# Low parts of the second layer's query and gate weights by ScalarE and an adding transfer, and the rotary swap by ScalarE

## The chip, the cores and the metric

The kernel runs on one core of a Trainium2 chip. A core has a matrix engine (TensorE, PE in the profile, with its weight loads as PEld), a vector engine (VectorE, DVE), an activation engine (ScalarE, ACT), a general engine (GpSimd, POOL), a queue engine that starts transfers (SyncE, SP) and 16 DMA engines. Each engine works through its own instructions in order; semaphores tie them together. Tiles lie in SBUF (128 partitions), matmul results in PSUM, inputs and outputs in HBM.

The metric is the time of one execution in microseconds (us), the median of several runs. A profiled execution gives the trace; its span runs from the first to the last instruction.

## The reference

Two layers work on x, 1024 tokens of 1024 features, each ending in a weighted residual and a layer norm. The first is gated linear attention with four heads. The second projects one shared set of keys and values and then, for eight query heads and three groups, runs attention over a dilated window:

```
for u in 0..7:                       # query heads, 128 wide
    for g, (window, d) in ((128,1), (512,4), (2048,16)):
        q = rope(x @ wB[u, g])       # 1024 tokens x 128
        k, v = K[u // 4, g], V[u // 4, g]
        o[g], lse[g] = attention of token t over t, t-d, t-2d, ..., t-window
    o = sum over g of o[g], weighted by softmax(lse over g)
    og[u] = o * silu(x @ wB[u, 3])
out = layer_norm(alpha * x + concat(og) @ wOB)
```

where rope(q) = q * cos + swap(q) * sin, and swap exchanges the two halves of the 128 features, with a minus sign on one of them. Everything is fp32.

## The kernel before

**Numbers in two parts.** A projection is made of fp32r matmuls, a format with fewer bits that TensorE multiplies faster (512 columns in 227 ns, where 128 of plain fp32 take 112 ns). A number is split into a high part, its rounding to fp32r, and a low part, what is left; a product is high*high + high*low + low*high. `mm3` (line 642) issues these three matmuls, `proj_cols` (649) eight times three for one half (512 tokens) of a projection, `project` (655) both halves for one piece of weights and hands each finished PSUM bank to an evacuation function.

**Weights.** A piece is 128 by 1024 numbers, 512 KB. `load_w` (625) starts its transfer on SP into `wf` (two buffers), ACT copies it to the high part `wh` (three buffers), and DVE or GpSimd subtracts `wf - wh` into the low part `wl` (three buffers). There are 100 pieces of this full size, 32 of them from wB (queries and gates of the eight heads).

**The second layer** (`layer_b`). First values and keys are projected; then for each head `q_proj` (three pieces, rotated by `rope`), `g_proj` (one piece, silu through a tanh), `scores` and `attend`. `rope` (1194) makes acc * cos on DVE, two products of 64 partitions each on DVE for the swapped halves with sin, and one add on DVE or GpSimd that writes the result in the group's order (`to_group`): group 0 in token order, group 1 as four interleaved sequences of 256, group 2 as sixteen of 64. In `scores` (1327) a block of 128 queries is the stationary operand and the keys are the moving one; group 1 has per head four products 128 wide and four 256 wide. These score products are plain fp32. The exponentials run on ACT; the merge weights of the groups (`cw`) go through small DMAs; `attend` (1415) scales P, transposes it (into `ms`), masks it into `PT` (DVE, and in part GpSimd), and multiplies by V into `po`.

**What sets the order.** The program is recorded first and then put in order by a planner of its own (`Sched`, lines 141 to 454), which also chooses the engine where the code leaves a choice: `S.vp` is DVE or GpSimd, `S.va` DVE or ACT, `S.vap` any of the three. It places operation after operation by a modelled start time and a priority, with costs from `cost` (543 to 595); loads of weights are recorded with a priority that places them early. So a change to costs or to a choice moves instructions on every engine. All of them are issued from one line, 452 (453 after the change), so the profile's groups are told apart by tiles, not lines.

Of the kernel before, what the change touches and what calls it, by code (L numbers as in the profile page):

```python
# [12 lines left out]
AF = mybir.ActivationFunctionType  # L13
# [21 lines left out]
WEIGHTS, EVAC, WARM = 3000, 1000, 4  # L35
AHEAD = 0.35
RUNS, GATHER = 0.3, 1.0


class Buf:  # L40
# [100 lines left out]
class Sched:  # L141
# [20 lines left out]
    def record(self, engs, meth, args, kw):  # L162
        a = list(args)
        outs = [v for k, v in kw.items() if k in ("out", "accum_out")]
        ins = [v for k, v in kw.items() if k not in ("out", "accum_out")]
        if "out" not in kw:
            outs.append(a[0])
            ins = a[1:] + ins
        else:
            ins += a  # L170
        outs = [v for v in outs if isinstance(v, View)]
        ins = [v for v in ins if isinstance(v, View)]
        if meth == "copy_predicated":
            ins += outs
        n = max([int(_np.prod(v.shape[1:])) for v in outs + ins if not (meth == "matmul" and v is not outs[0])] or [0])
        func = None
        if meth in ("copy", "affine", "scale"):
            func = "Copy"
        elif meth == "activation":
            func = str(a[2]).split(".")[-1]  # L180
        costs = [cost(e, meth, n, outs, ins, args, kw) + self.extra for e in engs]
        g = self.group_op
        if g is None:
            o = Op()
            o.engs, o.calls, o.reads, o.writes, o.cost = engs, [], [], [], [0.0] * len(engs)
# [12 lines left out]
        o.reads += ins  # L198
        o.writes += outs
        o.cost = [x + y for x, y in zip(o.cost, costs)]  # L200
# [53 lines left out]
    def order(self):  # L254
# [62 lines left out]
        while n_done < len(ops):  # L317
# [40 lines left out]
                    c += 1.3 if cur_set else 0.0  # L358
                    cur_set = new
            o.t0, o.eng = st, e  # L360
            if e == "SP":
                dma_free = max(dma_free, st) + c
                o.t1 = dma_free + 1.7
                free[e] = st + 0.37
            else:
                o.t1 = st + c
                free[e] = o.t1
                if o.port[o.engs.index(e)]:
                    port = o.t1
# [162 lines left out]
def shares_port(e, meth, outs, ins):  # L532

    n = sum(v.buf.pool.space is None for v in ins if int(_np.prod(v.shape[1:])) > 1)
    if e == "POOL":
        return n > 0
# [6 lines left out]
def cost(e, meth, n, outs, ins, args, kw):  # L543

    if e == "PE":
# [9 lines left out]
            return 0.12  # L555
        m = args[1].shape[1]
        return {32: 0.02, 64: 0.05}.get(m, 0.43)
    if e == "SP":
# [39 lines left out]
def trunk(tc, xT, wP, wA, wA12, wAv3, w2, wO, wK, wV0, wV12, wB, wOB, par_d,  # L598
# [23 lines left out]
        return slice(half * 512, half * 512 + 512)  # L622


    def load_w(src):
        with S.later(-WEIGHTS):
            return load_w_now(src)

    def load_w_now(src):
# [6 lines left out]
        split_hi(hi, wf)  # L636
        lo = wts.tile([128, 1024], FR, name="wl", bufs=3)
        lo = lo[:, :k * c].rearrange("p (k c) -> p k c", k=k)
        split_lo(lo, wf, hi)
        return hi, lo  # L640

    def mm3(acc, wh, wl, xh, xl, kt):
# [9 lines left out]
            xh, xl = xs[kt]  # L652
            mm3(acc, hi[:, kt, :], lo[:, kt, :], xh[:, r], xl[:, r], kt)

    def project(piece, xs, evac, halves=(0, 1)):
        w = load_w(piece)
# [519 lines left out]
    def layer_b(xs, early):  # L1176
# [14 lines left out]
        sinT = page(p0, F32, "sinT")  # L1191
        S.sync.dma_start(sinT, sin_d)

        def rope(pg, g, half, acc):
            r = hs(half)
            t1 = small("t1", "t1", 2)
            S.vector.tensor_mul(t1, acc, cosT[:, r])
            t2 = small("t2", "t2", 2)
            S.vector.tensor_mul(t2[0:64, :], acc[64:128, :], sinT[64:128, r])
            S.vector.tensor_mul(t2[64:128, :], acc[0:64, :], sinT[0:64, r])  # L1200
            S.vp.tensor_add(to_group(pg, g, half), tok_view(t1, g), tok_view(t2, g))

        K = [[page(p0, F32, f"K{c}{g}") for g in range(3)] for c in range(2)]
        V = [[None] * 3 for _ in range(2)]
# [98 lines left out]
        def q_proj(u):  # L1303
            Q = [page(p0, F32, "Q") for _ in range(3)]
            U[u]["Q"] = Q
            for g in range(3):
                project(wB[u, g], xs, lambda half, acc: rope(Q[g], g, half, acc))


        def g_proj(u):  # L1310
# [7 lines left out]
            project(wB[u, 3], xs, evac)  # L1318


        def pieces(P, g, j0):
# [4 lines left out]

        def scores(u):
            Q, Kc = U[u]["Q"], K[u // 4]
            P = {}
            sts = hp.tile([128, 2, 24], F32, name="sts", bufs=2)  # L1330
            for g in (2, 1, 0):
                step = 8 if g == 2 else 2
                for j0 in range(0, 8, step):
# [11 lines left out]
                    for j in range(j0, j0 + step):  # L1345
# [4 lines left out]
                        P[g, j] = p, o  # L1350
                        px = p[:, o:o + nk]
                        if g < 2:
                            S.tensor.matmul(sc[:, o:o + nk], Q[g][:, qc:qc + 128], Kc[g][:, kc:kc + nk],
                                             start=True, stop=True)
                        mk = rmask if g == 2 else bmask[:, 256 - nk:]

# [244 lines left out]
def _arrays(inputs):  # L1601
# [10 lines left out]
    r = np.arange  # L1612
# [36 lines left out]
    a["sin"] = c(np.concatenate([sn, -sn]))  # L1649
# [36 lines left out]
```

## Time and profile before

| | |
|---|---|
| runs | 1154.63, 1153.87, 1154.25 us; median 1154.25 |
| profiled execution | span 1152.7 us; the median lies 1.55 us above it |
| granted TensorE clock | 0.998 of full speed |
| transfers | 107.13 MB on the hardware queue, 29.6% of 16 DMA engines |
| a transfer of GpSimd's queue | none |

The profile lists busy times by engine, the share of each engine in 40 slices, the chain of work that ended last, and groups of equal instructions. In a group `wl<-wf,wh 128x1024` reads: result, operands, shape; `x39` is the count, then total busy time, mean ns of one, and the idle time before them with what ended it. The timeline has start, duration, engine, line, instruction, with the idle time before it and its releaser in brackets. A matmul's duration is longer than the distance to the next one, since they are pipelined; the distance counts.

### The profile page before, as it was taken

The page shows a single profiled execution, that of the slowest core. Times are in us where ns is not written, and L with a number is a line of the kernel's source. Part 1 is how long each engine was busy: PE and PEld are TensorE (multiplying, and loading weights), DVE is VectorE, ACT ScalarE, POOL GpSimd, SP SyncE. Part 2 cuts the span into 40 slices and gives each one's busy share as a digit, 9 for nine tenths or more (in the row PEclk, how much of TensorE's full clock was granted, in tenths as well). Part 3 has the DMA queues.
Part 4 walks back from the last instruction along what each step waited for, and adds up shares of the span by engine and source line. Part 5 has one row for each costly group of instructions (what it writes and reads, how often), then busy time and mean ns, then how long its engine had stood idle before and what let it go on. Part 6 is the DMA issues. An engine that isn't in the chain of part 4 may idle for free.

```text
span 1152.7 us, 19731 instructions
## 1 busy us (share of the span) xinstructions
PE 1142.8 (99%) x7780; PEld 975.2 (85%) x7780; DVE 820.3 (71%) x1634; ACT 449.1 (39%) x929; POOL 188.0 (16%) x139
## 2 busy tenths in 40 slices
PE   9999999999999999999999999999999999999997
PEld 9888888889988888888988888888888888888876
DVE  6286862786966699764366868686777878767678
ACT  5355431646463335311214242424222443444342
POOL 1000100112011120211020303030211312212200
PEclk9999999999999999999999999999999999999999
DMA  7211222111144365443611111121141111134544
GB/s 256 71 38 38 74 79 87 38 61 51 57 171 140 137 214 158 166 143 103 208 47 34 51 38 57 38 50 45 38 165 39 38 21 38 39 96 126 193 136 182
DMA packets 93372, 108.39 MB, mean 94 GB/s; under 512 B 43648, under 2 KB 61952, under 8 KB 93280
## 3 DMA queue, kind: packets, MB, share of 16 engines
q1 hardware_dynamic: 93280, 107.13, 29.6%
q8 instruction: 61, 1.00, 0.4%
q14 instruction: 31, 0.25, 0.1%
HBM read 85.94 MB, written 21.17 MB: 93 GB/s over the span
## 4 chain that ended last, share of the span: by engine, by line
PE 93%; DVE 4%; DMA 2%; ACT 1%; issue 1%; POOL 0%; DVEq 0%; ACTq 0%
PE acc L452 63%; PE po L452 9%; PE lv L452 8%; PE vac L452 7%; PE ms L452 4%; PE pro L452 2%; DMA wf<-in_wOB 2%; DVE rt L452 1%; DVE wl L452 1%; DVE x1l L452 0%; ACT wh L452 0%; DVE P L452 0%; DVE lnA L452 0%; ACT woh L452 0%; DVE wol L452 0%
## 5 line engine op out<-in xcount | busy, mean ns | idle before, releaser
L452 PE MATMUL acc<-x1h,wh 128*128 128x512 f32 x608 | 252.3, 415 | 0.0
L452 PE MATMUL acc<-x1h,wl 128*128 128x512 f32 x608 | 237.6, 391 | 0.0
L452 PE MATMUL acc<-x1l,wh 128*128 128x512 f32 x608 | 237.1, 390 | 0.0
L452 ACT ACTIVATE wh<-wf 128x1024 fp32r<-128x1024 f32 (+2 forms) x104 | 108.1, 1040 | 281.0 <-PE acc L452 194.8
L452 POOL TENSOR_TENSOR wl<-wf,wh 128x1024 fp32r<-128x1024 f32 x39 | 93.5, 2397 | 553.1 <-ACT wh L452 414.8
L452 ACT ACTIVATE P<-P,sts 128x128 f32<-128x128 f32 (+2 forms) x192 | 81.5, 426 | 139.6 <-DVE sts L452 139.3
L452 PEld LDWEIGHTS acc<-x1h,wl 128*128 128x128 f32 x608 | 114.1, 188 | 24.5
L452 PEld LDWEIGHTS acc<-x1l,wh 128*128 128x128 f32 x608 | 114.5, 188 | 21.3
L452 PEld LDWEIGHTS acc<-x1h,wh 128*128 128x128 f32 x608 | 114.4, 188 | 21.1
L452 DVE TENSOR_TENSOR wl<-wf,wh 128x1024 fp32r<-128x1024 f32 (+2 forms) x66 | 83.4, 1265 | 58.2 <-ACT wh L452 48.0
L452 PE MATMUL acc<-xh,wh 128*128 128x512 f32 x256 | 101.8, 397 | 0.0
L452 PE MATMUL acc<-xh,wl 128*128 128x512 f32 x256 | 99.8, 390 | 0.0
L452 PE MATMUL acc<-xl,wh 128*128 128x512 f32 x256 | 99.7, 390 | 0.0
L452 DVE TENSOR_TENSOR t<-acc,cosT 128x512 f32<-128x512 f32 x60 | 41.4, 689 | 65.7 <-PE acc L452 65.7
L452 DVE TENSOR_TENSOR t<-acc,sinT 64x512 f32<-64x512 f32 x120 | 82.5, 688 | 1.6
L452 PE MATMUL lv<-K,Q 128*64 128x64 f32 (+2 forms) x512 | 70.2, 286 | 0.0
L452 DVE CUSTOM_DVE_ANT_0 P<-lv,bmask 128x256 f32<-128x256 f32 (+1 forms) x128 | 46.7, 379 | 25.1 <-PE lv L452 23.7
L452 PEld LDWEIGHTS lv<-K,Q 128*128 128x128 f32 (+1 forms) x512 | 53.8, 163 | 10.0 <-issue 1.6
L452 PE MATMUL acc<-ogh,wh 128*128 128x512 f32 x152 | 60.1, 395 | 0.0
L452 PE MATMUL acc<-ogh,wl 128*128 128x512 f32 x152 | 59.2, 389 | 0.0
L452 PE MATMUL acc<-ogl,wh 128*128 128x512 f32 x152 | 59.2, 389 | 0.0
L452 PEld LDWEIGHTS acc<-xh,wl 128*128 128x128 f32 x256 | 48.0, 188 | 10.2
(252 smaller groups left out, 2233.4 us busy)
## 6 DMA issues: line engine op xcount, KB each, us to landing
wf<-in_wB SPq DMA_DIRECT2D x32, 512.0 KB
wf<-in_wA SPq DMA_DIRECT2D x24, 512.0 KB
wf<-in_wO SPq DMA_DIRECT2D x16, 512.0 KB
wf<-in_wOB SPq DMA_DIRECT2D x16, 512.0 KB
wf<-in_wV SPq DMA_DIRECT2D x12, 512.0 KB
res<-in_xT SPq DMA_DIRECT2D x16, 256.0 KB
x1d<-rt SPq DMA_DIRECT2D x16, 256.0 KB
out<-rt SPq DMA_DIRECT2D x16, 256.0 KB
```

What stands on the lines that cost most here:

```text
L452: getattr(handle[o.eng], meth)(*[conv(a) for a in args], **{k: conv(v) for k, v in kw.items()})
```

## The change

Four things change.

1. For the 32 pieces of wB the low part is no longer a subtraction. ACT writes the negated high part into `wl` (a copy of `wf` with scale -1, rounded to the same format), and a transfer on GpSimd's queue reads the same piece from HBM a second time and adds it to `wl`.
2. In `rope`, ACT copies the two halves of the PSUM bank, swapped, to `t2`, and one product with sin of all 128 partitions follows on DVE or GpSimd. The signs in the sin array are exchanged to suit. This holds for the keys as well.
3. Group 1 of the queries is stored in token order; `scores` reads its blocks with a step of four elements (16 bytes) as the stationary operand.
4. The planner gets costs for such transfers: 1.1 us of GpSimd (`ISSUE`) and 3.0 us until landing (`QUEUED`), and treats the target of an adding transfer as an input.

```diff
-            if e == "SP":
+            if o.calls[0][0] == "dma_start":
                 dma_free = max(dma_free, st) + c
-                o.t1 = dma_free + 1.7
-                free[e] = st + 0.37
+                o.t1 = dma_free + (1.7 if e == "SP" else QUEUED)
+                free[e] = st + (0.37 if e == "SP" else ISSUE)
...
         lo = lo[:, :k * c].rearrange("p (k c) -> p k c", k=k)
-        split_lo(lo, wf, hi)
+        if added:
+            S.scalar.activation(lo, wf, AF.Copy, scale=-1.0)
+            S.gpsimd.dma_start(lo, src, accum_op=OP.add)
+        else:
+            split_lo(lo, wf, hi)
...
-        def rope(pg, g, half, acc):
+        def rope(pg, g, half, acc, walked=(0, 1, 2)):
...
-            S.vector.tensor_mul(t2[0:64, :], acc[64:128, :], sinT[64:128, r])
-            S.vector.tensor_mul(t2[64:128, :], acc[0:64, :], sinT[0:64, r])
-            S.vp.tensor_add(to_group(pg, g, half), tok_view(t1, g), tok_view(t2, g))
+            S.scalar.copy(t2[0:64, :], acc[64:128, :])
+            S.scalar.copy(t2[64:128, :], acc[0:64, :])
+            S.vp.tensor_mul(t2, t2, sinT[:, r])
+            if g in walked:
+                S.vp.tensor_add(to_group(pg, g, half), tok_view(t1, g), tok_view(t2, g))
+            else:
+                S.vp.tensor_add(pg[:, r], t1, t2)
...
-                project(wB[u, g], xs, lambda half, acc: rope(Q[g], g, half, acc))
+                project(wB[u, g], xs, lambda half, acc: rope(Q[g], g, half, acc, (0, 2)), added=True)
...
+            Q = [Q[0], Q[1].rearrange("p (i r) -> p r i", r=4), Q[2]]
...
-                            S.tensor.matmul(sc[:, o:o + nk], Q[g][:, qc:qc + 128], Kc[g][:, kc:kc + nk],
+                            qb = Q[1][:, qc // 256, qc % 256:qc % 256 + 128] if g else blk(Q[0], j)
+                            S.tensor.matmul(sc[:, o:o + nk], qb, Kc[g][:, kc:kc + nk],
```

The planner places the second layer anew. On GpSimd, from the last rows of the first layer to the first head's attention; `x1l` is the low part of that layer's result, `PT` the masked attention weights. Before:

```order
L452 TENSOR_TENSOR x1l_4390<-rt,x1h_4373 128x512
L452 TENSOR_TENSOR x1l_4445<-rt,x1h_4430 128x512
L452 TENSOR_TENSOR wl<-wf,wh 128x1024 x12
L452 TENSOR_SCALAR P<-P,cw 128x256 x3
L452 TENSOR_TENSOR wl<-wf,wh 128x1024
L452 TENSOR_TENSOR Q<-t_6224,t_6236 128x4x8x16
L452 TENSOR_TENSOR PT<-P,ident 128x128
L452 TENSOR_TENSOR PT<-P,ident 128x256 x3
```

The same place after:

```order
L453 TENSOR_TENSOR x1l_4390<-rt,x1h_4373 128x512
L453 TENSOR_TENSOR x1l_4445<-rt,x1h_4430 128x512
L453 TENSOR_TENSOR wl<-wf,wh 128x1024 x6
L453 DMA wl<-in_wB 128x1024 x9
L453 TENSOR_TENSOR PT<-P,ident 128x128 x3
L453 DMA wl<-in_wB 128x1024
L453 TENSOR_TENSOR PT<-P,ident 128x128
L453 TENSOR_TENSOR PT<-P,ident 128x256 x3
```

GpSimd keeps its masked products and a few subtractions of key and value weights; where it subtracted for queries and gates, it issues transfers, and the scaling of P and the add into Q have left it.

On ACT, in the queries of the second head while the first head's scores end; `P,sts` is an exponential with its sum, `ew` belongs to the merge weights, `t` is a half of the swap. Before:

```order
L452 ACTIVATE th<-acc 128x512
L452 ACTIVATE P,sts<-P,sts 128x256 x6
L452 ACTIVATE wh<-wf 128x1024
L452 ACTIVATE ew<-ew 128x24
L452 ACTIVATE wh<-wf 128x1024
L452 ACTIVATE P<-P,cw 128x128
```

The same place after:

```order
L453 ACTIVATE P,sts<-P,sts 128x256 x6
L453 ACTIVATE t_6022<-acc 64x512 x2
L453 ACTIVATE P,sts<-P,sts 128x256
L453 ACTIVATE wh<-wf 128x1024
L453 ACTIVATE wl<-wf 128x1024
L453 ACTIVATE t_6077<-acc 64x512 x2
L453 ACTIVATE ew<-ew 128x24
L453 ACTIVATE t_6124<-acc 64x512 x2
L453 ACTIVATE wh<-wf 128x1024
L453 ACTIVATE wl<-wf 128x1024
```

Each high part has its negation behind it, and each half projection two copies that empty its PSUM bank.

On PE, at the first head's attention; `ms` are transposes, `lv` scores, `po` the products with V. Before:

```order
L452 MATMUL po<-diag,V_5481 128x128 x8
L452 MATMUL ms<-ident,P 128x128 x8
L452 MATMUL lv<-K_5174,Q 64x64 x16
L452 MATMUL po<-PT,V_5401 128x128 x2
L452 MATMUL lv<-K_5008,Q 128x128
L452 MATMUL po<-PT,V_5401 128x128 x10
L452 MATMUL ms<-ident,P 128x128 x4
L452 MATMUL po<-PT,V_4656 128x128
```

The same place after:

```order
L453 MATMUL po<-diag,V_5497 128x128 x8
L453 MATMUL ms<-ident,P 128x128 x8
L453 MATMUL lv<-K_5180,Q 64x64 x16
L453 MATMUL po<-PT,V_5413 128x128 x12
L453 MATMUL lv<-K_5010,Q 128x128
L453 MATMUL po<-PT,V_4656 128x128
```

The score product of group 1 (`K_5008` before, `K_5010` after) stands behind the whole run of products with V instead of inside it, and one group of transposes has gone ahead of the place shown; the products themselves are the same in number and shape.

More of the change, by code (lines that the diff above doesn't have):

```diff
@@ L37 @@
 RUNS, GATHER = 0.3, 1.0
+QUEUED, ISSUE = 3.0, 1.1
 class Buf:
@@ L172, in record @@
         ins = [v for v in ins if isinstance(v, View)]
-        if meth == "copy_predicated":
+        if meth == "copy_predicated" or "accum_op" in kw:
             ins += outs
@@ L535, in shares_port @@
     if e == "POOL":
-        return n > 0
+        return n > 0 and meth != "dma_start"
     if e != "DVE":
@@ L557, in cost @@
         return {32: 0.02, 64: 0.05}.get(m, 0.43)
-    if e == "SP":
+    if meth == "dma_start":
         return 0.1 + int(_np.prod((outs + ins)[0].shape)) * 4 / 280e3
@@ L622, in hs, with load_w, load_w_now @@
         return slice(half * 512, half * 512 + 512)
-    def load_w(src):
+    def load_w(src, added=False):
         with S.later(-WEIGHTS):
-            return load_w_now(src)
-    def load_w_now(src):
+            return load_w_now(src, added)
+    def load_w_now(src, added):
         k, c = src.shape[1], src.shape[2]
@@ L653, in proj_cols, with project @@
             mm3(acc, hi[:, kt, :], lo[:, kt, :], xh[:, r], xl[:, r], kt)
-    def project(piece, xs, evac, halves=(0, 1)):
-        w = load_w(piece)
+    def project(piece, xs, evac, halves=(0, 1), added=False):
+        w = load_w(piece, added)
         for half in halves:
@@ L1317, in evac @@
                 S.vector.scalar_tensor_tensor(sg[:, hs(half)], th, 1.0, acc, op0=OP.add, op1=OP.mult)
-            project(wB[u, 3], xs, evac)
+            project(wB[u, 3], xs, evac, added=True)
         def pieces(P, g, j0):
@@ L1648, in _arrays @@
     a["cos"] = c(np.concatenate([cs, cs]))
[L1649 removed]
+    a["sin"] = c(np.concatenate([-sn, sn]))
     q, k = np.meshgrid(r(128), r(256), indexing="ij")
```

## Prediction

> **What bounds the kernel now.** I read the page first: the busy shares, the 40 slices, and the engines' shares of the chain that ended last.
>
> ```profile
> PE 1142.8 (99%) x7780; PEld 975.2 (85%) x7780; DVE 820.3 (71%) x1634; ACT 449.1 (39%) x929; POOL 188.0 (16%) x139
> PE   9999999999999999999999999999999999999997
> PE 93%; DVE 4%; DMA 2%; ACT 1%; issue 1%; POOL 0%; DVEq 0%; ACTq 0%
> ```
>
> TensorE (PE) is busy in 1142.8 of 1152.7 us, in every slice at 90% or more except the last, and is 93% of the chain. VectorE (DVE) is the next at 71%, GpSimd (POOL) has 16%. A busy PE may still be slowed from outside, so I then read the waits of PE and, in the chain of waits, how long its runs take.
>
> ```profile
> PE pro L452 <- DVE Dg L452: 1.2, 1, 1.2
> PE po L452 <- DVE PT L452: 0.8, 1, 0.8
> PE ms L452 <- DVE sum L452: 0.5, 2, 0.2
> PE ms L452 <- ACT sum L452: 0.2, 1, 0.2
> ```
> ```profile
> 510.23 10.92 PE acc L452 x48
> 804.84 28.61 PE acc L452 x126
> 1142.65 2.89 PE lv L452 x24
> ```
>
> PE waits four kinds of times, 2.7 us together. The first is in the first layer, which the change leaves alone; the second is the one wait of PE on an engine in the second layer's heads; the last two belong to layer norms. A projection matmul costs 28.61 / 126 = 227 ns in the middle of the heads and 10.92 / 48 = 227 ns between the K pieces: it does not depend on what DVE does meanwhile. PE's last matmul ends at 1142.65 + 2.89 = 1145.5 us, and what follows to 1152.7 is the last layer norm and the store, not touched. So PE waited 1145.5 - 1142.8 = 2.7 us, which agrees with the list.
>
> One stage, one head in the middle of the second layer (61 us), by the windows; the columns are the sum and PE, PEld, DVE, ACT, POOL, then clock, DMA share and GB/s:
>
> ```profile
> 726.00:787.00 61.00, 61.00 (x349) 52.41 (x348) 45.24 (x118) 21.34 (x70) 13.14 (x11) 1.00 0.17 45
> ```
>
> PE is busy in all of it; DVE has 15.8 us free, ACT 39.7, GpSimd 47.9, the DMA engines 83%. What takes work from DVE here gives PE nothing unless PE waits somewhere for DVE, and what adds work to ACT or GpSimd costs nothing unless it makes PE wait.
>
> **The change, part by part.** PE's instructions are the same ones as before; their order differs only from the first head's scores on. The sum is therefore the waits of PE that go, the waits that come, and any matmul or load whose own time changes.
>
> *Low parts of 32 weight pieces (24 of queries, 8 of gates).* Removed is one subtraction each; added are one ACT copy and one accumulating transfer of 512 KB.
>
> ```profile
> L452 ACT ACTIVATE wh<-wf 128x1024 fp32r<-128x1024 f32 x100 | 105.7, 1058 | 280.9 <-PE acc L452 194.8 <-issue 44.1 <-PE vac L452 30.1
> L452 POOL TENSOR_TENSOR wl<-wf,wh 128x1024 fp32r<-128x1024 f32 x39 | 93.5, 2397 | 553.1 <-ACT wh L452 414.8 <-PE ms L452 117.6 <-PE lv L452 12.1
> L452 DVE TENSOR_TENSOR wl<-wf,wh 128x1024 fp32r<-128x1024 f32 x61 | 80.4, 1319 | 58.2 <-ACT wh L452 48.0 <-PE ms L452 9.7
> ```
>
> Before, the low part is there 1.06 (high part) + 1.32 (DVE) or 2.40 (GpSimd) = 2.4 to 3.5 us after the buffer comes free. The negation is the same shape and engine as the high part, 1.06 us. No trace row shows a transfer of GpSimd's queue or one that adds. Its nearest rows are the plain loads of the same 512 KB:
>
> ```profile
> 1081.90 4.35 DMA wf<-in_wOB
> 1088.63 4.25 DMA wf<-in_wOB
> 1095.24 5.08 DMA wf<-in_wOB
> ```
>
> Lower end 4.25 us (adding is free), upper end twice the slowest, 10.2 us (the target is read as well). GpSimd's own share of issuing: from 0 to the 2.40 us of the subtraction that it replaces. New chain: 1.06 + 1.06 + (0 to 2.40) + (4.25 to 10.2) = 6.4 to 14.7 us; I take 10, since nothing else presses on the DMA engines here (17%). When it is due is read from ACT's timeline at the turn from one head to the next:
>
> ```profile
> 689.66 1.06 ACT L452 ACTIVATE wh<-wf 128x1024 fp32r<-128x1024 f32 x1 [5.55 <-PE acc L452]
> 700.59 1.06 ACT L452 ACTIVATE wh<-wf 128x1024 fp32r<-128x1024 f32 x1 [6.02 <-PE acc L452]
> 711.42 1.06 ACT L452 ACTIVATE wh<-wf 128x1024 fp32r<-128x1024 f32 x1 [5.31 <-PE acc L452]
> ```
>
> The copies follow one another by 10.9 us, one piece of PE work, each released by PE as it leaves a piece: there are three buffers, so a piece that starts to load then is needed two pieces later, after 2 x 10.9 = 21.8 us. That is the cover: 14.7 at most against 21.8, and 7.1 us are left. Cost at PE: 0. If the cover were gone (a chain of 24 us), each piece would cost about 2 us.
>
> The Trainium skill ("SBUF — State Buffer", section "SBUF: two separate sides", its warning on GpSimd-queue transfers) speaks against this part: GpSimd writes the transfer's descriptors, and a VectorE copy between SBUF operands in a fast mode can lock it out, with an example of about 620 ns alone growing to 3100 ns. No row of this trace shows such a transfer; by that example the estimate of the issue would be five times as long, at most 12 us instead of 2.4, and the chain 24 us instead of 14.7.
>
> *Rope swap on ACT.* Six half pieces of queries a head (and twelve of keys ahead of the heads) are rotated. Removed are two DVE products in each; added are two ACT copies and one product on DVE or GpSimd.
>
> ```profile
> L452 DVE TENSOR_TENSOR t<-acc,sinT 64x512 f32<-64x512 f32 x120 | 82.5, 688 | 1.6
> L452 ACT ACTIVATE th<-acc 128x512 f32<-128x512 f32 x16 | 9.4, 588 | 20.6 <-PE acc L452 20.6
> L452 DVE TENSOR_TENSOR rt<-rt,R 128x512 f32<-128x512 f32 x24 | 16.0, 683 | 0.3 <-ACT R L452 0.3
> ```
>
> Per head DVE loses 12 x 0.688 = 8.3 us and gains at most 6 x 0.683 = 4.1; ACT gains 12 x 0.588 = 7.1, and with four negations 4.2, so 21.3 + 11.3 = 32.6 of 61 us. What can matter is how soon a finished PSUM bank is emptied, since PE has two and needs the next after 5.45 us (half of 10.9). Before: 3 x 0.69 = 2.1 us on DVE. After, in the worst place, ACT first makes high part and negation and then both copies: 1.06 + 1.06 + 2 x 0.588 = 3.3 us, below 5.45. Behind these ACT instructions stand the softmax exponentials of the same head; PE's next use of them is a piece or more away. Cost at PE: 0.
>
> *Group 1 of the queries stays in token order.* The add's stride goes; in its place 64 stationary loads (8 a head) step by 16 bytes. This is the one edit that changes an instruction of PE. Rows of PE's timeline for steps of 16 bytes on its other side (first row: group 1, its results written by steps of 16 bytes; the others contiguous), and the score matmuls:
>
> ```profile
> 720.35 2.40 PE L452 MATMUL po<-PT,V 128*128 128x128 f32 x20
> 725.31 3.29 PE L452 MATMUL po<-PT,V 128*128 128x128 f32 x28
> ...
> L452 PE MATMUL lv<-K,Q 128*128 128x128 f32 x80 | 15.9, 280 | 0.0
> 737.43 0.59 PE L452 MATMUL lv<-K,Q 128*128 128x256 f32 x2
> L452 PE MATMUL lv<-K,Q 128*128 128x256 f32 x176 | 49.9, 379 | 0.0
> ```
>
> With 0.28 us for the last one's full time, a step is (2.40 - 0.28) / 19 = 112 ns and (3.29 - 0.28) / 27 = 111 ns: a 16-byte step into PSUM costs nothing. A 256-wide one steps by 0.59 - 0.379 = 0.21 us. Reading a stationary operand by such steps has no row; the row against it is DVE's add of group 1, which writes by large steps:
>
> ```profile
> 692.01 1.73 DVE L452 TENSOR_TENSOR Q<-t,t 128x512 f32<-128x512 f32 x1
> ...
> 698.60 1.09 DVE L452 TENSOR_TENSOR Q<-t,t 128x512 f32<-128x512 f32 x1
> ```
>
> 1.09 us against 0.683 contiguous is a factor of 1.6. So a load takes 1.0 to 1.6 times its contiguous time. With a load of up to 112 ns (it keeps pace with 112 ns steps), the stepped one is 112 to 179 ns. Behind a projection matmul (227) or a 256-wide one (0.21 us) it hides. Behind a 128-wide one, 67 ns show. By the order, at most four of a head's eight loads stand behind one: 32 loads, 0 to 2.1 us; were all 64 exposed, 4.3 us. Nothing excludes a gain outright, but none of the rows shows a stepped access faster than a contiguous one. I take 0, by the row of the same engine.
>
> The Trainium skill ("SBUF — State Buffer", section "Door 1: The DMA port swizzle (why `[64,N]` ≈ `[32,N]`)", its note on cachelines) says that SBUF is served in 16-byte lines with a penalty for each access that crosses into a new line, and that for PSUM any non-contiguous pattern slows matmuls significantly. The trace disagrees on PSUM (112 against 111 ns) and shows no row for the SBUF half; by that rule these 64 loads pay, which is the first rival.
>
> *Order.* GpSimd's order now has transfers where it had subtractions, and DVE's small products move; PE's own order changes shape less often. What such a change costs is seen where PE comes from attention products into a projection run:
>
> ```profile
> 723.17 0.48 PE L452 MATMUL acc<-x1h,wh 128*128 128x512 f32 x1
> 723.48 0.40 PE L452 MATMUL acc<-x1l,wh 128*128 128x512 f32 x1
> 723.71 0.39 PE L452 MATMUL acc<-x1h,wl 128*128 128x512 f32 x1
> ```
>
> The first step is 0.31 us, the next 0.23: 0.08 us for a change. Counted in the order, there are 27 changes fewer between the 128- and 256-wide products and 4 more entries into projection runs, so this lies between 27 x -0.08 = -2.2 and 4 x 0.08 = +0.3 us. The attention runs above have no first step that stands out, so I take -0.2.
>
> *Sum.* 1152.7 + 0 (weights) + 0 (swap) + 0 (loads) - 0.2 = 1152.5 us of span. The runs' median of 1154.25 lies 1.55 us above the profiled span, so 1154.0 us. The measurement can tell about 0.2% from no change, 2.3 us: 1151.9 to 1156.6 count as the same.
>
> **The rivals.**
>
> *1. The stepped loads show (slower).* Mechanism: place and price as above, decided at a load time above 112 ns. At 1.6 times, 1154.25 + 2.1 = 1156.4 us for the 32 and 1158.5 for all; at twice, 32 x 112 ns = 3.6 us gives 1157.9. For it: DVE's factor of 1.6, and that PE has no free time in which it could be absorbed. Against it: steps in PSUM cost PE nothing. The smaller price would just count as the same, the others as slower. Chance that it counts as slower: 0.17.
>
> *2. The accumulated low parts come too late (slower).* GpSimd works through its queue in order; a transfer that waits for ACT's negation holds the masked products of the attention (PT) behind it, for which PE has one wait already, with 0.77 us:
>
> ```profile
> 702.13 3.98 ACT L452 ACTIVATE P<-P,cw 128x128 f32<-128x128 f32 x11 [0.48 <-DMA cw<-cwd]
> 711.45 1.03 PE L452 MATMUL ms<-ident,P 128*128 128x128 f32 x8
> ...
> 1053.79 0.40 PE L452 MATMUL acc<-ogh,wl 128*128 128x512 f32 x1
> 1054.95 3.13 PE L452 MATMUL po<-PT,V 128*128 128x128 f32 x24 [0.77 <-DVE PT L452]
> ```
>
> The merged weights of a head arrive 9 us ahead of PE's use (702.1 to 711.4), so a hold of a few us hides there; the last head has no such room. It decides where a chain passes 21.8 us, or a hold 9 us. Price: 24 - 21.8 = 2.2 us for each late piece; if 8 of 32 are late, 18 us and 1172. Against it: 7.1 us left over and GpSimd free for 47.9 of 61 us. Chance 0.08.
>
> *3. PE loses its last waits (faster).* The lighter DVE removes the wait at 1054.95 (1.16 us from start to start instead of 0.23, so 0.9 us), and the new order the 2.2 us of shape changes at most: 1154.25 - 3.1 = 1151.1 at best, 1153.3 when only the first holds, which would count as the same. Past 0.2% both are needed. Chance 0.07.
>
> That the change does not do what it says has no own time: if the transfers were not taken out of PE's way or DVE not relieved, PE would be fed as before, and the forecast is the same.
>
> **How the numbers follow.** Forecast 0.68: 1154.0 us, its own range 1152.0 to 1156.4 (the shape changes at their best, the 32 loads at 1.6 times). The three rivals have 0.17, 0.08 and 0.07. Faster by over 0.2% is rival 3, 0.07; slower is rivals 1 and 2, 0.25; the same 0.68. The range runs from 1152.0 to 1158.5, which takes in the forecast and rival 1 up to its full price at a factor of 1.6; left out are rival 2, rival 3 and the factor of two and more, together about 0.18.
>
> **What would show it.** Right: PE's busy time within 3 us of 1142.8, no new line among PE's waits, score matmuls of group 1 still 112 and 210 ns apart, DVE's window some 4 us lighter and ACT's at about 33 of 61. Rival 1: the same number of loads with a mean above the present one and PE's score runs longer by 67 ns a pair. Rival 2: a wait of PE for a transfer into the low part, or for PT. I am wrong in the mechanism if the time moves by over 2.3 us with PE's waits and loads unchanged.

## The result, and the profile after

| | before | after |
|---|---|---|
| median of the runs | 1154.06 us (1153.64 to 1154.63, 4 runs) | 1164.55 us (1161.77 to 1167.0, 4 runs) |
| ratio to before | | 1.0092, 95% interval 1.0075 to 1.0109 |
| span of the profiled execution | 1152.7 us | 1163.7 us |

The change is slower by 10.5 us, where no change was forecast. Also new is the spread: 5 us between runs of after, 1 us between runs of before. The profiled execution of after is one of its longer ones (1165.48 us), so its parts add up to somewhat more than the medians. The page of after, its busy times and its two big DMA queues:

```profile
PE 1152.1 (99%) x7780; PEld 987.2 (85%) x7780; DVE 755.7 (65%) x1596; ACT 540.6 (46%) x1057; POOL 148.4 (13%) x141
...
q1 hardware_dynamic: 93280, 107.13, 30.3%
q0 software_dynamic: 4608, 16.78, 8.2%
```

The kernel is as bound by PE as it was, DVE lost 64.6 us of work and ACT gained 91.5, and PE is busy for 9.3 us longer with the same 7780 instructions. So most of the loss stands inside PE's own instructions, not in its waits. One head of after, from the same place to the same place of the next one (before, the columns being those of the prediction, then after):

```profile
743.92:804.84 60.92, 60.92 (x347) 52.33 (x347) 45.24 (x118) 21.26 (x68) 13.14 (x11) 1.00 0.17 45
```
```profile
746.26:808.18 61.92, 61.92 (x347) 53.53 (x347) 38.93 (x116) 30.95 (x80) 7.43 (x11) 1.00 0.36 78
```

ACT moved as the prediction said (30.95 us), DVE somewhat more (6.3 us less instead of some 4), PE waits for nothing, and the head is still 1.00 us longer. Eight heads give 8 us. Where it sits is seen in the groups of weight loads and of score products, before and after:

```profile
L452 PEld LDWEIGHTS lv<-K,Q 128*128 128x128 f32 x256 | 45.7, 189 | 7.7
```
```profile
L453 PEld LDWEIGHTS lv<-K,Q 128*128 128x128 f32 x256 | 57.0, 253 | 6.2
...
L453 PE MATMUL lv<-K,Q 128*128 128x256 f32 x176 | 49.4, 387 | 0.0
L453 PE MATMUL lv<-K,Q 128*128 128x128 f32 x80 | 20.5, 348 | 0.0
```

The mean load grew from 189 to 253 ns. Half of the 256 are in group 1, so the stepped ones take 2 x 253 - 189 = 317 ns. They are 128, not 64: each plain fp32 product appears in the trace as two matmuls with a load each. In PE's timeline the row of before is a group 1 product of two such matmuls, the first row of after is the same with stepped loads, and the second is two stepped products 256 wide:

```profile
720.13 0.39 PE L452 MATMUL lv<-K,Q 128*128 128x128 f32 x2
```
```profile
859.36 0.50 PE L453 MATMUL lv<-K,Q 128*128 128x128 f32 x2
860.41 1.08 PE L453 MATMUL lv<-K,Q 128*128 128x256 f32 x4
```

Less the last one's full time (0.28 and 0.38 us), the steps are 0.11 us before, 0.22 stepped, and 0.23 for the 256-wide, which took 0.21. So in both rows a stepped load follows the one before it by 0.22 to 0.23 us, whether that one belongs to a 128-wide or to a 256-wide product.

The rest is a new wait. The waits of PE, after:

```profile
PE ms L453 <- DVE P L453: 2.3, 2, 2.0
PE pro L453 <- DVE Dg L453: 1.3, 1, 1.3
PE po L453 <- DVE PT L453: 0.3, 1, 0.3
PE ms L453 <- ACT sum L453: 0.2, 1, 0.2
PE ms L453 <- DVE sum L453: 0.2, 1, 0.2
```

The first line was not there. PE wants to transpose the P that the merge weights have scaled, and it is late in heads 4 and 5. The 2.0 us cost more than 2.0 us, as PE's timeline and the windows around it show (the seventh number of a window is the granted clock):

```profile
888.58 0.39 PE L453 MATMUL acc<-x1h,wl 128*128 128x512 f32 x1
890.94 0.83 PE L453 MATMUL ms<-ident,P 128*128 128x128 f32 x4 [1.98 <-DVE P L453]
891.42 0.78 PE L453 MATMUL acc<-x1h,wh 128*128 128x512 f32 x1
892.00 0.63 PE L453 MATMUL acc<-x1l,wh 128*128 128x512 f32 x1
892.42 0.63 PE L453 MATMUL acc<-x1h,wl 128*128 128x512 f32 x1
```
```profile
888.50:891.00 2.50, 0.52 (x4) 0.10 (x3) 2.04 (x11) 2.12 (x3) 0.00 (x0) 1.00 0.00 0
891.00:895.00 4.00, 4.00 (x13) 3.28 (x14) 3.10 (x5) 1.94 (x4) 0.86 (x1) 0.57 0.64 100
```

Behind the wait the matmuls go at 427 instead of 227 ns for about 3 us, at a granted clock of 0.57 in that window: some 1.5 us more. The chain of waits and SP's queue of after show what came last before P:

```profile
880.95 7.04 DMA nat<-std
...
1153.53 2.89 PE lv L453 x24
```
```profile
877.94 1.64 SPq L453 DMA_DIRECT2D nat<-std  x2
879.93 0.35 SPq L453 DMA_DIRECT2D wf<-in_wB  x1
880.32 1.26 SPq L453 DMA_DIRECT2D nat<-std  x2
```

The last gather of the heads' statistics (`nat`, 2 KB) lands 7.04 us after its issue, with a weight load issued in the middle of the four. In head 1 of the same run, with no load among them, DVE's first reader of the gathers (`mnB`) starts 1.1 us after the four issues end (688.50 + 2.69 = 691.19). The four issues in head 1, then the two readers, in head 1 and in head 4:

```profile
688.50 2.69 SPq L453 DMA_DIRECT2D nat<-std  x4
```
```profile
692.32 0.17 DVE L453 TENSOR_TENSOR mnB<-nat 128x8 f32<-128x8 f32 x1 [1.75 <-DMA nat<-std]
...
887.98 0.17 DVE L453 TENSOR_TENSOR mnB<-nat 128x8 f32<-128x8 f32 x1 [0.56 <-DMA nat<-std]
```

In head 4, however, DVE stood idle for the gather for only 0.56 us; until then it was busy with the rotation of the next head's queries. A gather in time would have brought P 0.56 us forward, so about 1.4 of the 1.98 us have another holder, DVE's own queue. The swap alone, below, shows what holds that up.

The books: PE busy 9.3 us more, of which the runs below put 8.0 on the stepped loads; the other 1.3 fit the half-speed matmuls; PE idle 1156.4 (1153.53 + 2.89, the last row of the chain above) - 1152.1 = 4.3 us up to its last matmul instead of 2.7; together 10.9 of the 11.0 us between the spans.

### The profile page after: what moved, and what is told of

It reads as the page before. It is cut to its first block, busy times and chain, and to the rows that moved or that the text cites. A ratio compares the mean times of both kernels' runs of the same rounds, so it can differ in the third digit from the quotient of the medians.

```text
span 1163.7 us, 19926 instructions
## 1 busy us (share of the span) xinstructions
PE 1152.1 (99%) x7780; PEld 987.2 (85%) x7780; DVE 755.7 (65%) x1596; ACT 540.6 (46%) x1057; POOL 148.4 (13%) x141
## 4 chain that ended last, share of the span: by engine, by line
PE 94%; DVE 3%; DMA 1%; ACT 0%; issue 0%; SPq 0%; DVEq 0%; ACTq 0%
PE acc L453 61%; PE lv L453 10%; PE po L453 9%; PE vac L453 7%; PE ms L453 4%; PE pro L453 2%; DMA nat<-std 1%; DVE rt L453 1%; DVE wl L453 1%; DVE x1l L453 0%; DVE PT L453 0%; DVE lnA L453 0%; SPq L453 0%; ACT wh L453 0%; ACT wl L453 0%
## 5 line engine op out<-in xcount | busy, mean ns | idle before, releaser
L453 ACT ACTIVATE t<-acc 64x512 f32<-64x512 f32 x120 | 71.1, 592 | 85.5 <-DVE t L453 74.8
L453 DVE TENSOR_TENSOR wl<-wf,wh 128x1024 fp32r<-128x1024 f32 (+2 forms) x60 | 76.0, 1269 | 53.4 <-ACT wh L453 43.5
L453 DVE TENSOR_TENSOR t<-t,sinT 128x512 f32<-128x512 f32 x53 | 43.1, 814 | 61.9 <-ACT t L453 61.8
L453 PE MATMUL lv<-K,Q 128*64 128x64 f32 (+2 forms) x512 | 78.4, 300 | 0.0
L453 PEld LDWEIGHTS lv<-K,Q 128*128 128x128 f32 (+1 forms) x512 | 65.1, 195 | 8.0 <-issue 0.8
L453 POOL DMA_DIRECT2D wl<-in_wB x32 | 27.9, 873 | 307.7 <-ACT wl L453 285.5
L453 POOL TENSOR_TENSOR wl<-wf,wh 128x1024 fp32r<-128x1024 f32 x13 | 31.0, 2387 | 223.9 <-PE ms L453 117.6
```

The lines of the kernel that those rows point to most:

```text
L453: getattr(handle[o.eng], meth)(*[conv(a) for a in args], **{k: conv(v) for k, v in kw.items()})
```

## The experiments

Times are medians beside runs of the kernel before on the same chip, which lie between 1153.7 and 1154.5 us. Theory A at the start: the loads cost 8 us, the late P with the slow matmuls 3 to 4.

**The loads, by one pair in each of two orders.** The changed kernel with group 1's blocks read as contiguous columns, so that its scores use the wrong queries and every order stays (an excerpt, like the diffs below):

```diff
-                            qb = Q[1][:, qc // 256, qc % 256:qc % 256 + 128] if g else blk(Q[0], j)
+                            qb = Q[g][:, qc:qc + 128]
```

> The changed kernel, every engine's order the same, but the group 1 query blocks are read as contiguous columns (wrong queries for that group's scores; only the time is read). Theory A (two causes: 128 stepped loads of 318 instead of 189 ns cost about 1 us a head, 8 us; late small transfers and the slow matmuls behind a stall cost 3 to 4 us): 1164.5 - 8 = 1156.5 us, PE waits for the weighted P in two heads as before. Rival B (the loads hide, all of the loss is waits and transfers): 1164.5 us.

Measured: 1157.71 us, ratio 1.0030 (1.0019 to 1.0042); PE busy 1144.1 us instead of 1152.1, all loads 180 to 200 ns long. The waits stay, and grow a little, since PE comes to them sooner:

```profile
PE ms L453 <- DVE P L453: 3.1, 3, 2.0
PE pro L453 <- DVE Dg L453: 1.2, 1, 1.2
PE po L453 <- DVE PT L453: 0.7, 1, 0.7
```

So the loads cost 6.8 us at the end and 8.0 us of busy PE, and 3.7 us have another cause. The six runs of this kernel also show the clock: three have a mean granted clock of 0.999 and take 1155.5 to 1156.8 us, three have 0.996 or 0.997 and take 1158.6 to 1159.3.

The kernel before with only the third part of the change (the token order of group 1, shown here, and the stepped read as in the change):

```diff
-                project(wB[u, g], xs, lambda half, acc: rope(Q[g], g, half, acc))
+                project(wB[u, g], xs, lambda half, acc: rope(Q[g], g, half, acc, (0, 2)))
```

> The kernel before with group 1 of the queries in token order and the stepped loads, and nothing else. Theory A: 1154 + 8 = 1162 us, no new wait of PE on another engine, 128 loads of about 318 ns. Rival B: 1154 us.

Measured: 1163.65 us, ratio 1.0089 (1.0076 to 1.0102). Two more kernels have exactly this one's order on every engine. In one, group 1 steps by two elements instead of four; in the other, group 0 steps by four as well (both with wrong queries):

```diff
-            Q = [Q[0], Q[1].rearrange("p (i r) -> p r i", r=4), Q[2]]
+            Q = [Q[0], Q[1].rearrange("p (i r) -> p r i", r=2), Q[2]]
```

> The kernel before with group 1 in token order and its blocks read with a step of two elements, 8 bytes, instead of four (wrong queries for that group's scores; only the time is read), every engine's order the same as with the 16-byte step (1163.65 us). Theory F (what costs is a read that uses each 16-byte line once): 8 bytes use each line twice, 1154 to 1155 us. Rival G (any step costs the same): 1163.6 us; a cost in proportion to the bytes walked over would give some 1157.

```diff
-            Q = [Q[0], Q[1].rearrange("p (i r) -> p r i", r=4), Q[2]]
+            Q = [q.rearrange("p (i r) -> p r i", r=4) for q in Q[:2]] + [Q[2]]
```

> The kernel before with stepped loads in group 1, and the group 0 query blocks read with the same 16-byte step as well (wrong queries for that group's scores; only the time is read), every engine's order the same as with group 1 alone (1163.65 us). Theory A (a stepped load holds PE to one product in 235 ns): 16 more loads a head, 14 behind 256-wide products (215 to 235 ns) and 2 behind narrower ones (112 to 235): 0.5 us a head, 1168 us. Rival D (each stepped load costs a fixed 70 ns): 8 x 16 x 70 ns = 9 us, 1172.6 us. Rival E (they hide behind 256-wide products): 1165.5 us.

Measured: 1157.08 us with a step of 8 bytes, 1166.54 with both groups at 16. The three groups of loads, with 8 bytes, with 16 in one group, with 16 in both:

```profile
L452 PEld LDWEIGHTS lv<-K,Q 128*128 128x128 f32 x256 | 46.2, 192 | 8.4 <-DVE sts L452 1.3
```
```profile
L452 PEld LDWEIGHTS lv<-K,Q 128*128 128x128 f32 x256 | 56.7, 254 | 6.6 <-DVE sts L452 0.8
```
```profile
L452 PEld LDWEIGHTS lv<-K,Q 128*128 128x128 f32 x256 | 66.6, 317 | 3.8 <-DVE sts L452 0.8
```

With 8 bytes a load is as long as a contiguous one, with 16 it is 317 ns. The time of 1157.08 us alone would also fit a cost in proportion to the bytes walked over (some 1157), but the loads exclude it: 192 ns against 189. Theory F holds as far as these two steps can show it: not the step as such but the read that uses 16 bytes once is dear; steps between them or above were not run. The price in one order is 1163.65 - 1157.08 = 6.6 us for 128 loads, 51 ns each; the next 128, which stand mostly behind 256-wide products, add 2.9 us, 23 ns each. (The 16-byte kernel ran beside a before of 1154.06 us and the other two beside one of 1154.47; each less its own before, the prices are 7.0 and 2.5 us.) A fixed price (1172.6) is ruled out. Between theory A (1168) and rival E (1165.5, all hidden behind 256-wide products) the 1166.54 lies nearer to E; that the hiding is not complete rests on the 0.23 instead of 0.21 us between 256-wide products, shown above. The 8-byte kernel's own 2.6 us over before are then put down to the order: the edit moves DVE's and GpSimd's adds, and the planner places the rest anew (the control for that comes below).

**The other two parts alone.** The kernel before with the adding transfer alone, and with the swap alone:

> The kernel before with the negated high part and the adding transfer (and the planner's costs for it), and nothing else. Theory A, if the adding transfers alone hold up the small statistics transfers: a wait of PE for the weighted P in one or two of the heads 4 to 7, 1155 to 1158 us. Rival C (the swap on ACT and the order it brings hold them up): 1154 us, no such wait.

> The kernel before with the rotary swap by ACT, and nothing else. Theory A: 1154 us within 1, since ACT has 39 of 61 us free in a head. Rival C: 1156 to 1158 us, with the wait for the weighted P in heads 4 and 5.

Measured: 1159.91 us (1156.46 to 1162.09), ratio 1.0054 (1.0038 to 1.0070), and 1158.27 us, ratio 1.0042 (1.0030 to 1.0054). Each alone costs as much as both together without the stepped loads, or more, so they don't add up. The swap alone makes P late in heads 4, 5 and 6, against theory A's 1154 and as rival C said. PE's wait for it, and DVE's queue in head 4, which shows the cause:

```profile
PE ms L452 <- DVE P L452: 4.0, 3, 1.4
```
```profile
881.05 0.69 DVE L452 TENSOR_TENSOR t<-t,sinT 128x512 f32<-128x512 f32 x1 [1.33 <-ACT t L452]
881.77 1.11 DVE L452 TENSOR_TENSOR Q<-t,t 128x512 f32<-128x512 f32 x1
882.71 0.18 DVE L452 TENSOR_TENSOR mnB<-nat 128x8 f32<-128x8 f32 x1
```

DVE waits 1.33 us for ACT's copies, makes the product and the add, and goes on to the gathers' reader without any idle time. By the times at which the semaphores of the gathers rise in the trace, the last of them had landed at 880.77, although a weight load is issued in their middle here too. So P does not wait for the gathers here; DVE's queue, which ACT's copies hold up, is what makes it late. That there is no room for 1.33 us at this place is a matter of the order, as the next runs show.

The adding transfer's profiled execution, at 1156.46 the fastest of its six, shows one such wait of 1.0 us, in head 6, and there DVE is idle for the gathers; what its runs at 1162 wait for was not caught in a profile.

**More room in the plan.** If the planner only underrates the gathers, a longer landing time in its model should open a gap. The same one-line edit, at 5.0 in the changed kernel without stepped loads and in the swap alone, then at 2.0 and 1.5:

```diff
-RUNS, GATHER = 0.3, 1.0
+RUNS, GATHER = 0.3, 5.0
```

> The changed kernel with group 1 written and read as before, so without stepped loads, and the planner's landing time of the small gathers raised from 1.0 to 5.0 us (so that it leaves more PE work ahead of the weighted P). Theory A: the waits for the weighted P come from a chain of small transfers that is longer than the planner leaves room for; they go, 1154 us within 1.5. Rival C (the added work of ACT and of the DMA engines costs PE by itself): 1157 us or more, as with contiguous loads in the planned order (1157.7).

> The rotary swap by ACT alone with the planner's landing time of the small gathers at 5.0 us. Theory A: the three waits of the swap alone (4.0 us, 1158.3 us) go, 1154 us within 1.5. Rival C: 1158 us.

Measured: 1213.41 and 1180.79 us, both far worse. The largest wait of PE in the first:

```profile
PE ms L453 <- DVE P L453: 33.4, 5, 12.0
```

The constant does not add room to one place. It moves the whole second layer, here to an order in which PE waits for P up to 12 us. Neither theory is tested by that. The smaller values, and the kernel before with 2.0 as the control:

> The rotary swap by ACT alone with the planner's landing time of the small gathers at 2.0 us instead of 1.0 (5.0 had moved far more than the room). Theory A (the planner puts the first use of the weighted P some 1.4 us too early in heads 4 to 6): the three waits shrink or go, 1154 to 1156 us against 1158.3. Rival C (the added ACT work costs PE by itself): 1158 us or more.

> The changed kernel with group 1 written and read as before, so without stepped loads, landing time at 2.0 us. Theory A: the waits for the weighted P and the half-speed matmuls behind the longest go, 1154 to 1155.5 us against 1157.7 in the order with 1.0. Rival C: 1157 us or more with the waits elsewhere.

> The same with 1.5 us. Theory A: the longest wait falls below about 1.5 us, so that no matmul runs at half speed behind it: 1155 to 1156.5 us. Rival C: 1157.7 us.

> The kernel before with 2.0 us and nothing else, as the control: what another order of the second layer is worth without any of the change. Theory A: 1153 to 1155 us, since before has no wait for the weighted P to lose. Rival H (any other order of the planner costs a few us, whatever the cause): 1156 us or more.

Measured: 1156.07, 1157.49, 1157.04 and 1157.26 us (ratios 1.0012, 1.0027, 1.0023, 1.0025, the last with 1.0016 to 1.0034). The swap alone loses most of its waits for P (0.7 us are left), and of its 4.2 us over before 1.7 are left. The control loses 2.9 us with nothing of the change in it: rival H. The old order is a well-chosen one, and a kernel that makes the planner leave it starts behind, here by some 2 to 3 us.

**The work in the old order.** To part order from work, the planner is given the old operations, and where one of them is issued, the new ones are issued in its place, so that PE's and SP's order are those of before. For the swap, the first of the two marked products issues an ACT copy, the second an ACT copy and then the DVE product with sin:

```diff
-            S.vector.tensor_mul(t2[0:64, :], acc[64:128, :], sinT[64:128, r])
-            S.vector.tensor_mul(t2[64:128, :], acc[0:64, :], sinT[0:64, r])
+            S.vector.tensor_mul(instead(lower, first), acc[64:128, :], sinT[64:128, r])
+            S.vector.tensor_mul(instead(upper, second), acc[0:64, :], sinT[0:64, r])
```

> The swap by ACT put into the order of the kernel before: the planner plans the old products, and in their places the two ACT copies and then one DVE product are issued; PE's and SP's order are those of before. Theory H (what the swap alone lost, 4.2 us, is the new order): 1154 us within 1, no wait for the weighted P. Rival C (the work itself costs PE): 1157 us or more.

> The negated high part and the adding transfer in the places of the old subtractions, PE's and SP's order those of before. Theory H: 1154 to 1155 us. Rival C (the adding transfer holds up the gathers behind the weight loads by 1 to 2 us, which heads 4 to 6 have no room for): waits for the weighted P, 1156 to 1159 us.

> Both in the order of before, without stepped loads. Theory H: 1154 to 1155.5 us, against 1157.7 with both in the planner's new order. Rival C: 1157 us or more.

> The whole change in the order of before, stepped loads too. The loads cost 6.6 to 6.9 us in two pairs of kernels of one order each. Theory H: 1154.5 + 6.9 = 1161 to 1162 us. Rival C: 1164 us or more, as the change in its own order.

Measured: 1166.93, 1156.26 (ratio 1.0020, 1.0011 to 1.0029), 1180.58 and 1186.31 us. Theory H is wrong for the swap. In an order that is not made for it, it costs 12.6 us. The waits of PE and DVE's products of that kernel:

```profile
PE lv L463 <- DVE sts L463: 6.3, 6, 2.2
PE po L463 <- DVE diag L463: 1.9, 4, 0.5
```
```profile
L1217 DVE TENSOR_TENSOR t<-t,sinT 128x512 f32<-128x512 f32 x60 | 63.6, 1060 | 93.7 <-ACT t L1216 93.7
```

DVE stands 93.7 us waiting for ACT's copies, and the score reductions (`sts`), for which PE now waits 6.3 us, stand in the same queue behind these waits. The rope used to be DVE's alone; now each half goes from DVE to ACT and back. In after the planner's new order lowers this, but not to nothing:

```profile
L453 DVE TENSOR_TENSOR t<-t,sinT 128x512 f32<-128x512 f32 x53 | 43.1, 814 | 61.9 <-ACT t L453 61.8
```

For the adding transfers theory H is nearly right: in the old order PE has no wait for P at all and 2.0 us are lost; where, was not found. The last pair gives the loads a third time: 1186.31 - 1180.58 = 5.7 us.

**The weight load among the gathers.** In heads 4 to 6 the new order has SP issue a weight load in the middle of the last four gathers; the old order has it behind them. Only these loads are moved behind, all other engines keep their order:

```diff
         self.end = max(o.t1 for o in ops)
-        return done
+        return gathers_first(done)
```

> The changed kernel without stepped loads (group 1 written and read as before; PE's and SP's order as in the run with contiguous columns, 1157.7 us), and in heads 4 to 7 the weight load that SP issues in the middle of the last four small gathers is issued behind them; every other engine's order is the same. Theory K (the gathers land 6 to 7 us after their issue because a 512 KB load is ahead of them in SP's queue, and that makes the weighted P late): last gather to first use falls from 7 to 2 to 3 us in heads 4 to 6, the waits for the weighted P and the half-speed matmuls go, 1154 to 1155.5 us. Rival L (the adding transfer on GpSimd's queue holds them up wherever they stand): 1157 us or more.

> The whole change, stepped loads too, with the same move of the weight loads behind the last gathers in heads 4 to 7 and nothing else. Theory K: 1164.5 less 2 to 4 us, 1160.5 to 1162.5, no wait for the weighted P over 0.3 us. Rival L: 1164 us or more.

Measured: 1155.92 us, ratio 1.0018 (1.0009 to 1.0027), without the stepped loads, and 1162.33 us, ratio 1.0074 (1.0060 to 1.0087), with them. The second differs from after in SP's queue alone: 8.6 us over its before instead of 10.5, so 1.9 us back. The first has PE's order of the kernel with contiguous columns, but other orders on ACT, DVE and GpSimd: 2.2 us over before instead of 3.7. The intervals of each pair overlap, so these sizes are rough; the traces are clearer. The waits of PE, then SP's and DVE's queue in head 4, with the stepped loads:

```profile
PE ms L453 <- DVE P L453: 1.3, 1, 1.3
PE pro L453 <- DVE Dg L453: 1.3, 1, 1.3
```
```profile
877.51 3.14 SPq L453 DMA_DIRECT2D nat<-std  x4
880.75 0.57 SPq L453 DMA_DIRECT2D wf<-in_wB  x1
```
```profile
885.15 0.69 DVE L453 TENSOR_TENSOR t<-t,sinT 128x512 f32<-128x512 f32 x1 [1.32 <-ACT t L453]
885.88 1.10 DVE L453 TENSOR_TENSOR Q<-t,t 128x512 f32<-128x512 f32 x1
886.81 0.17 DVE L453 TENSOR_TENSOR mnB<-nat 128x8 f32<-128x8 f32 x1
```

One wait of 1.3 us is left of two, no matmul runs at half speed behind it, and the runs lie within 1.7 us of each other instead of 5. Theory K's times came out nearly, 1155.92 us just above its range and 1162.33 inside it; its two other signs did not. The wait of 1.3 us that stays has the holder that the swap alone showed: DVE waits for ACT's copies and goes from the add to the reader without idle time, and the gathers have all landed before, at 885.59 by their semaphores. Nor do the gathers land in 2 to 3 us. The time from the issue of the last gather to its landing, read in the same way in heads 4 to 6, is 2.4 us in before (neither a load nor an adding transfer issued among them), 2.8 to 3.1 in the swap alone (a weight load), 6.3 to 7.2 in after (a load and an adding transfer), and with the load moved behind, the adding transfer still among them, 5.4 to 5.6 with the stepped loads and 5.5 to 6.1 without. So a load among the gathers costs them little by itself; most of the delay comes with the adding transfer, which is rival L's mechanism.

None of the 18 kernels is faster than before; the nearest by ratio are the swap alone at 2.0 us (1156.07) and the swap and adding transfers with the gathers first (1155.92).

## Why the prediction was wrong

**What failed first: the price of the stepped loads.** The prediction took 0 by "the row of the same engine", PSUM written by 16-byte steps, and gave rival 1 a chance of 0.17 with 2.1 to 4.3 us. The mechanism was rival 1's; two terms of it were too small. The count: "64 stationary loads (8 a head)" were products, and the rows it quoted beside them had 80 + 176 = 256 matmuls for 128 products, so two loads each, 128 in group 1. The factor: it let a load grow by 1.6, from 112 to 179 ns, because a DVE write had (the 1.09 us; the row of 1.73 us beside it is group 0's contiguous add, which says nothing of steps), and left the factor of two that it named out of its range; the distance grew to 0.22 to 0.23 us, a factor of 2, and 256-wide products no longer hide it wholly. Measured in one order: 6.6 and 6.8 us. The page of the Trainium skill that the prediction weighed ("SBUF — State Buffer", section "Door 1: The DMA port swizzle (why `[64,N]` ≈ `[32,N]`)") names a condition on SBUF that fits the runs, two uses of a 16-byte line: 192 ns a load at 8 bytes, 317 ns at 16. Its half on PSUM was refuted by a row, and that was taken as evidence against the other half. It was none: that row is of results written to PSUM, and the question was of operands read from SBUF.

**What failed second: "a hold of a few us hides there; the last head has no such room".** The slack of 9 us was read at the turn from head 1 to head 2 and carried to all heads but the last. In before, the gate pieces of heads 4 to 7 are left to the end (their tanh runs from 989 us on), and in heads 4 to 6 little stands between P and its use. In head 4 P is ready at 892.53 + 0.69 = 893.22 and used at 893.86:

```profile
892.53 0.69 DVE L452 TENSOR_TENSOR P<-P,cw 128x512 f32<-128x512 f32 x1
```
```profile
893.86 0.60 PE L452 MATMUL ms<-ident,P 128*128 128x128 f32 x4
```

That is 0.64 us of room; heads 5 and 6 have 1.07 and 0.33, heads 1 to 3 have 14.9. After leaves none: PE comes to P too early by 1.98 us in head 4 and by 0.30 in head 5. Rival 2 named P's holders as GpSimd's queue; it was DVE's queue, which waits for ACT, and in part the statistics gathers on SP's queue, for which DVE stood idle for 0.56 us in head 4, 0.94 in head 5 and 0.48 in head 6 of after.

**What failed third: "Cost at PE: 0" for the swap.** The times were right (592 ns a copy, 30.95 us of ACT in a head for 32.6 forecast). Left out was the new dependency: DVE's queue stops at a product until ACT has copied, 61.8 us in all, and what stands behind it in the queue is late with it, the readers of the gathers and so P. In the swap alone that is 4.0 us of PE's waits in three heads.

**What held.** The low parts: a chain of 1.06 + 1.04 + 0.87 + 7.7 = 10.7 us against 10 forecast and 21.8 of cover, and PE never waits for them. The group and the issue's median landing time:

```profile
L453 POOL DMA_DIRECT2D wl<-in_wB x32 | 27.9, 873 | 307.7 <-ACT wl L453 285.5 <-ACT Vn L453 21.2 <-ACT V L453 1.0
```
```profile
wl<-in_wB POOLq DMA_DIRECT2D x32, 512.0 KB, 7.7
```

GpSimd's part took 0.87 us of the 0 to 2.40 given (the longest of the 32 took 1.02); the lock-out of which the Trainium skill warns ("SBUF — State Buffer", section "SBUF: two separate sides") does not show in these rows. Also right: what binds (PE), and that a relieved DVE gives PE nothing.

What was not foreseen is what an adding transfer does to small gathers in flight (6.3 to 7.2 us to landing instead of 2.4).

**The sum now.** Stepped loads 6.6 to 6.8 us; the rest 3.7 us. Of the rest 1.4 to 1.9, by two pairs of medians that are close to their noise, went when the gathers were issued ahead of the load, and with them the half-speed matmuls behind the longest wait; the wait of 1.3 us that stayed is DVE's queue waiting for ACT's copies. What is left, up to 1 us, is not placed. How much of the rest another order could hide is not settled: even the old kernel in another order lost 2.9 us. Nor is it settled what the longer runs of the adding transfer alone (1162 us) wait for.

## What to carry to other kernels

A strided read that is free for one engine and one memory has to be priced where it lands: on this kernel, which TensorE binds, a stationary operand with one fp32 in 16 bytes doubled the distance between loads, and the count is of loads in the trace, not of products in the source. Read the slack of a chain in every stage that has another mix of work, not in the one that is easiest to read. When a transfer seems late, look whether its reader was idle before it: a reader that comes straight from its engine's own work says nothing of when the data arrived. Where a planner sets the order, make a control in which only the order changes, since an edit is charged for both.

## What the runs showed of the hardware

- A 128-column fp32 load with 16-byte steps takes 317 ns in its record and follows the one before by 0.22 to 0.23 us, against 189 ns and 0.11 us contiguous; with 8-byte steps 192 ns.
- A pause of TensorE of 2.36 us from start to start (888.58 to 890.94) was followed by about 3 us of matmuls at 427 instead of 227 ns; the kernel with contiguous columns shows the same (883.25 to 885.61). The Trainium skill ("TensorE: Matmul & The Clock Gate", section "Part 1: The HAM clock gate (the "warmup" mystery)") sets the idle window at about 3.4 us, so here a shorter pause was enough; the pauses of 1.65 to 1.75 us in the runs with the gathers first and with the swap alone were followed by none.
- A gather of 2 KB landed 2.4 us after its issue with no bulk transfer issued among the four (before, heads 4 to 6), 2.8 to 3.1 with a 512 KB load among them (the swap alone), 5.4 to 6.1 with an adding transfer among them and the load behind, and 6.3 to 7.2 with both among them (after).
- An adding transfer of 512 KB from HBM into SBUF landed in 7.7 us (median of 32), 1.5 to 1.8 times the 4.25 to 5.08 of the plain loads that the prediction shows from before's last stage.
